# Gate vectors copied to all partitions by matmuls in place of GpSimd broadcasts, and small inputs loaded at the start

## The chip, the cores and the metric

The kernel runs on one core of a Trainium2 chip. The core has a tensor engine (PE; its weight loads are shown apart as PEld), a vector engine (DVE), a scalar engine (ACT), GpSimd (POOL) and a queue engine (SP) that here issues the large transfers. Each engine works through its own list of instructions in order and waits on semaphores for the others. The metric is the device time of one execution in microseconds.

## What is computed

256 tokens with 1024 channels, in float32, pass through two transformer blocks. The part that matters here is the modulation: six vectors of 1024 numbers for each layer come from a conditioning vector, and two of them are gates. A gate multiplies the result of a mixer or of a feed-forward network, channel by channel, before it is added to the tokens.

```python
mod = silu(c) @ w_ada + b_ada
sh1, sc1, g1, sh2, sc2, g2 = split(mod, 6)
x = x + g1 * mixer(modulate(x, norm1_g, sh1, sc1))
x = x + g2 * feed_forward(modulate(x, norm2_g, sh2, sc2))
```

The first block has one layer: a mixer of block attention and an mLSTM, then 32 experts. The second block has two layers: differential attention and then axial attention with grouped queries, each with a dense feed-forward network behind it. The differential attention needs one more number, lam, from four vectors of 64:

```python
lam = exp(sum(lq1 * lk1)) - exp(sum(lq2 * lk2)) + lam_init
```

## The kernel before

**Tiling.** Tokens lie on partitions in two tiles of 128; a product with weights takes activations transposed, 128 channels to a tile, and every operand is split in two exact halves, so that a float32 product is three matmuls (`mm3`). The halves of the activations are `hi` (ACT, line 593) and `lo` (POOL, line 596, from a tile `k` that DVE writes in line 595); those of the weights are `wh` (ACT, line 515) and `wl` (DVE, line 517), in at most four to six buffers. `dense` multiplies 512 columns of weights: eight steps of six matmuls into two banks of PSUM with the tag "g".

**Weights.** They come in units of 2 MiB, 5 slots in a ring, issued by SP in the order of use as slots come free (line 303). During the experts four further slots are there.

**Order of work.** Each engine's list is laid out at build time by a planner, which takes instructions by their place in the program text, lets one that is ready by its own model of the times go ahead of one that is not, and hands out buffers of a tag as they come free. Two calls bind it: `issue_after`, and `keep_in_program_order`, which pins an instruction behind the one that stands before it on the same engine in the text.

**Gates.** `gates` makes both gates of a layer in a tile `gm`: four rows, at partitions 0, 32, 64 and 96, with 512 numbers each, the other rows zero. `spread` copies each row to all 128 partitions, two rows for each gate, with four `partition_broadcast` instructions on POOL (line 497). It is called three times: in the first block, in layer 0 and in layer 1 of the second block, each time in `dense_work` between the mixer's products and `out_proj`, the product with the output weights, whose sums take all four banks "g". The gates are first read in `add_gated`, behind `out_proj` (lines 654 and 655). The first gate of the second block's layers stands in a buffer that held a value tile (`vh`, layer 0) or queries (`qT`, layer 1) before, and must wait for the attention's use of that. One more `partition_broadcast`, in line 1300, fills a gain for the experts' last group and is not touched.

**Layer 1 of the second block.** `axial_attention` has three products of 512 columns, for keys and values, and twice for queries. Behind each, `norm_rope` normalises the heads (line 1465 is the last to read the product's banks), rotates them (`rope_to`: products on DVE in lines 695 to 699, the sum and the difference on POOL in lines 697 and 700) and transposes them on PE (line 1474).

**Small inputs.** Five of the second block (`con_x`, `sub_g`, `lam`, `qk_g`, `grid`) are loaded by POOL in the middle of the first block (line 918), in text behind the mLSTM's gates. `lam` goes to all partitions, in a working tile of 1 KiB that must first come free; DVE sums the products on every partition (line 931), ACT takes the exponentials (line 933).

Of the kernel before, what the change touches and what calls it, by code (L numbers as in the profile page):

```python
# [19 lines left out]
T, D = 256, 1024  # L20
# [5 lines left out]
# columns of a unit of weights; the slots of their ring, and those beside it during the experts  # L26
UNIT = 4096
RING, RING2 = 5, 4
# the group of experts behind whose start the check for full queues comes
OVERFLOW_AT = 6  # L30
# how much of the mixers' attention goes beside their dense work, in steps more than there are: by layer of the second
# block; for the first block the steps of both
WEAVE = ((8, 0), (3, 0), (34, 52))
# (token tile, half) of the sums for GpSimd: of the second block, of the first
POOL_ADDS = ((0, 0), (1, 0))
POOL_A = ((0, 0),)
# how many splits stay behind the factors of a norm, by norm
BEHIND = (0, 4, 4, 0, 0)
# split weights held at a time, and the working tiles of the first mixer by size
AP, A1, A2 = 4, 6, 4  # L40
# shifts and scales computed with the vector engine: by layer and kind; the other modulation takes the tensor engine
COLS = ((0, 1), (1, 0), (1, 1))
# units of modulation after each unit of a mixer's weights, on the vector and on the tensor engine: of the first mixer,
# of the second
# [4 lines left out]
# the feed-forward network in two parts: their units of the first and of the second product  # L49
# [3 lines left out]
# columns of the constants: [128, C_N] for the whole program, [128, A_N] for the first block, [128, X_N] for the second  # L53
# [6 lines left out]
def constants():  # L60
    """Constants that depend on the shapes alone."""
# [30 lines left out]
def lay_out(i):  # L92
    """The inputs as the program reads them: slices, transposes and packing only."""
# [24 lines left out]
    def mcol(b, n1, n2):  # L118
        """biases of the shifts and scales and the gains, channels on partitions"""
        b = b.reshape(6, D)  # L120
        return np.concatenate([pc(b[0]), pc(b[1]), pc(n1), pc(b[3]), pc(b[4]), pc(n2)], 1)
# [7 lines left out]
    # outputs on rows: 512 of them to a unit  # L129
# [3 lines left out]
    # the first shift and scale by 256 channels: 128 shifts, their scales, and so on  # L133
# [28 lines left out]
    # by quarters of the columns  # L162
# [3 lines left out]
    # two heads' queries and keys to a unit, four heads' values  # L166
# [5 lines left out]
    o["lam"] = cc(np.concatenate([a["a_lam_q1_2"], a["a_lam_k1_2"], a["a_lam_q2_2"], a["a_lam_k2_2"]], 1))  # L172
# [12 lines left out]
def block_pair_kernel(ctx: ExitStack, tc: tile.TileContext, d, out):  # L185
# [12 lines left out]
    # working tiles by size: 1, 2 or 4 KiB to a partition  # L198
# [30 lines left out]
    # ---- the stream of weights: units of 2 MiB in the order of their use  # L229
# [51 lines left out]
    # the ring's slots: those of the last pool come first, and are the last before the second block's weights, which  # L281
    # wait for the first pool's
# [31 lines left out]
    # ---- constants and small inputs  # L314
    def bcast(src, offset, n):
        """n numbers of DRAM, the same on all partitions"""
        return bass.AP(tensor=src.tensor, offset=src.offset + offset, ap=[[0, 128], [1, n]])
# [14 lines left out]
    # the conditioning vectors  # L332
    se.activation(cs, cs, AF.Silu)

    def rsqrt(v, n):
        """1/sqrt(v), to float32's accuracy."""
# [4 lines left out]
        # with w = v y  # L341
# [15 lines left out]
    def rsqrts(vs):  # L357
        """1/sqrt(v) / RS for each v, one number a partition, to float32's accuracy."""
# [27 lines left out]
    def weave(*flows):  # L386
        """emits several flows (steps, their number) side by side"""
        live = [[0, n, steps] for steps, n in flows]
        while live:
            f = min(live, key=lambda f: (f[0] + 0.5) / f[1])  # L390
            f[0] += 1
            if next(f[2], live) is live:
                live.remove(f)

    def attention(n, ready, score, value, norm, turn, turn_ready=lambda: True):
        """steps of the attention by pairs of heads, each in n items: the scores of an item come ahead of the values of
        those before it, the transposition of a pair's result is put off behind scores of the next"""
# [26 lines left out]
    def ada(l, q, ps):  # L424
        """Two vectors of the modulation: psum rows 32j hold their pieces of 512"""
# [10 lines left out]
    def shift_scale(l, q, col, ps):  # L436
        """shift and gain * (1 + scale), channels on partitions: [128, 8 | 8]"""
# [10 lines left out]
    def ada_cols(l, q, cond, col):  # L448
        """a shift and a scale on the vector engine, outputs on partitions"""
# [12 lines left out]
    def cond_rows(b, dst):  # L462
        """a conditioning vector on all partitions"""
# [8 lines left out]
    def beside(steps, vfill, nv, fill, n_p):  # L472
        """8 steps with work of the modulation beside: units of the vector engine, and then those of the tensor engine"""
# [13 lines left out]
    def gates(l, m, ps):  # L487
        """the two gates, in rows 32j of m their pieces of 512"""
        po.memset(m, 0.0)
        po.dma_start(m[0:128:32, :], d["brow"][l])  # L490
        yield from ada(l, 2, ps)
        ve.tensor_add(m, ps, m)

    def spread(m, *gs):
        """the gates equal on all partitions"""
        for j in range(4):
            po.partition_broadcast(gs[j // 2][:, j % 2 * 512:(j % 2 + 1) * 512], m[32 * j:32 * j + 1, :])
# [6 lines left out]
    def behind():  # L504
        """the next splits are issued behind the norm's factors"""
# [5 lines left out]
    def split(w):  # L511
        """512 columns of weights as their two exact halves"""
# [7 lines left out]
    def mm3(ps, ah, al, bh, bl, first, last):  # L520
        """ps += a^T b, a and b in exact halves (the product of the two low halves is below float32's last place)"""
# [4 lines left out]
    def halves(tag="", pool=None):  # L526
        """activations, transposed, in exact halves: by 128 channels"""
        return tuple([mk(pool or parts[0], [128, T], F32R, f"{tag}{n}{k}") for k in range(DC)] for n in ("hi", "lo"))

    def dense(w, hi, lo, evict):  # L530
        """512 columns of weights: tokens on partitions"""
# [10 lines left out]
    def dense_t(w, hi, lo, evict, bank):  # L542
        """512 columns of weights: columns on partitions, 128 of them to a half bank"""
# [11 lines left out]
    def rows_into(w, ks, hi, lo, acc, first, last, lead=0, late=None):  # L555
        """acc[t][half] += a 128 rows of weights for each of ks, 1024 columns; the first tokens `lead` pieces ahead"""
# [21 lines left out]
    def turned(diag, evict, bank=psum, ks=range(0, DC, 2)):  # L578
        """the rows of x, each times its factor: evict(k, [128 channels, 256 tokens] in psum)"""
# [30 lines left out]
    def turn_into(hi, lo, gain, done, nh, k0=0):  # L610
        """a result, [128 tokens, t, nh, 128], to the exact halves of its transposes"""
# [10 lines left out]
    def out_proj(name, hi, lo, acc, done):  # L622
        """the product with a mixer's output weights, as the channels come"""
# [8 lines left out]
    def mean_square(src, junk):  # L632
        """one number a partition"""
# [4 lines left out]
    def diagonal(t, r, times):  # L638
        """the factors of 128 tokens on a diagonal"""
# [7 lines left out]
    def add_gated(t, acc, g, on_pool=POOL_ADDS, early=()):  # L647
        """x[t] += acc * g, by halves; its mean square, and EPS; in the tiles of the splits, but for `early` tokens, which come
        while those are in use"""
# [19 lines left out]
    def quotient_norm(v, den, nh, w, dst, ss=None):  # L669
        """v [128, nh, w] -> dst = v / den / rms(v / den), for den from 1 to the number of tokens; ss: sums of squares"""  # L670
# [5 lines left out]
    def head_norm(v, nh, w, dst, pre):  # L676
        """v [128, nh, w], times `pre` of each head -> dst = v / rms(v)"""
# [7 lines left out]
    def rope_to(dst, src, cs1, cs2, shape):  # L685
        """dst, src: (first halves, second halves); cs1, cs2: (cos, sin) for the first and for the second"""
# [15 lines left out]
    # =========================== first block, up to the experts ===========================  # L702
# [42 lines left out]
    # the conditioning vectors on all partitions, in the place of the gates that come later  # L745
# [3 lines left out]
    def modulated(u):  # L749
        """256 channels of the first modulation, and of the normalised tokens with it"""  # L750
# [14 lines left out]
    # queries and keys of the first attention: rotary embedding, transposed  # L765
# [8 lines left out]
    def store_k(dst, t, p2):  # L774
        """keys of two heads of 64 to a transposed tile, each with zeros in place of the other head"""
# [39 lines left out]
    def angles():  # L815
        """cos and sin of the given positions, arguments reduced to [-pi, pi]"""
# [24 lines left out]
    # the first product follows the channels as they come  # L841
# [21 lines left out]
    # gates of the mLSTM: heads on partitions, tokens along the free axis  # L863
# [5 lines left out]
    # rows h of these tiles are head h, the other rows stay zero  # L869
# [23 lines left out]
    # the running maximum that the second chunk starts from  # L893
# [12 lines left out]
    # as columns: [128 tokens, head]  # L906
# [9 lines left out]
    # small inputs of the second block  # L916
    def load(v, src):
        tc.keep_in_program_order(po.dma_start(v, src))
        return v

    con_x = load(mk(base, [128, X_CX], F32, "con_x"), d["const_x"][:, 0:X_CX])
    sub_g = load(mk(base, [128, 1], F32, "sub_g"), d["sub_g"])
    lamt = load(t1([128, 256]), bcast(d["lam"], 0, 256)).rearrange("p (a n) -> p a n", a=4)
    qk_g = load(mk(base, [128, 256], F32, "qk_g"), bcast(d["qk_g"], 0, 256)).rearrange("p (a n) -> p a n", a=2)
    grid = load(mk(base, [128, 256], F32, "grid"), d["const_x"][:, X_CX:X_N])

    LAM0 = 0.8 - 0.6 * math.exp(-0.3 * 0)
    ls = [mk(base, [128, 1], F32, f"ls{i}") for i in range(2)]
    for i in range(2):
        lj = t1([128, 64])  # L930
        ve.scalar_tensor_tensor(lj, lamt[:, 2 * i, :], 1.0, lamt[:, 2 * i + 1, :], op0=OP.mult, op1=OP.mult,
                                accum_out=ls[i])
        se.activation(ls[i], ls[i], AF.Exp)
    nlam = mk(base, [128, 1], F32, "nlam")
# [714 lines left out]
```

## Time and profile before

| | us |
|---|---|
| median of 3 runs | 1374.81 |
| lowest and highest | 1372.88 and 1378.33 |
| span of the profiled execution | 1375.5 |

The profile is of one execution, whose span, from its first to its last instruction, is 0.7 us above the median of the runs. Its page gives the busy time of each engine and a chain of work followed back from the end. [...] "issue" in brackets means that the engine waited for nothing that the profile shows.

### The profile page before, as it was taken

How to read it: one execution, taken by the hardware profiler on the slowest of the kernel's cores; microseconds unless marked ns; L12 is line 12 of the kernel's file. 1: busy time of each engine (PE TensorE's matmuls, PEld its weight loads, DVE VectorE, ACT ScalarE, POOL GpSimd, SP SyncE). 2: the span in 40 equal slices, each digit the busy share in tenths (PEclk: the TensorE clock that was granted, in tenths of full speed). 3: DMA queues.
4: the chain of work that ended last, by engine and by line, in shares of the span. 5: the costliest groups of instructions: out<-in, count | busy, mean ns of one | idle time of the engine just before them, and what ended most of it. 6: DMA issues, size and time to landing. Idle time of an engine off the chain costs nothing.

```text
span 1375.5 us, 19352 instructions
## 1 busy us (share of the span) xinstructions
PE 1116.8 (81%) x7505; PEld 813.4 (59%) x7505; DVE 680.8 (49%) x1598; ACT 485.4 (35%) x1046; POOL 160.6 (12%) x205
## 2 busy tenths in 40 slices
PE   5698998875656666575599999999995859999995
PEld 4486675421313222331377678989973646998994
DVE  7787896210202011111488777555553745655555
ACT  3254643100000000000356565554542525554552
POOL 2330000000000000000120103110123111310112
PEclk8799899978989897878899999999997989999998
DMA  9856887999999999989988739455365412844400
GB/s 389 352 200 254 339 316 327 429 425 426 425 428 427 426 427 425 424 363 428 425 329 319 279 120 373 181 192 198 149 255 211 180 61 107 338 184 184 184 32 31
DMA packets 29723, 397.51 MB, mean 289 GB/s; under 512 B 4156, under 2 KB 4556, under 8 KB 5560
## 3 DMA queue, kind: packets, MB, share of 16 engines
q1 hardware_dynamic: 28856, 395.22, 70.3%
q0 software_dynamic: 480, 0.96, 0.3%
q8 instruction: 61, 1.00, 0.3%
q14 instruction: 38, 0.31, 0.1%
q10 hardware_dynamic: 288, 0.02, 0.0%
HBM read 395.14 MB, written 1.05 MB: 288 GB/s over the span
## 4 chain that ended last, share of the span: by engine, by line
PE 39%; DMA 6%; DVE 5%; issue 4%; ACT 1%; POOL 1%; DVEq 0%; SPq 0%; ACTq 0%; POOLq 0%
PE b L524 6%; PE b L523 6%; PE b L522 6%; DMA w<-in_w_dram 6%; PE g L524 5%; PE g L522 5%; PE g L523 5%; DVE wl L517 1%; PE g L432 1%; PE b L1396 1%; PE b L585 1%; PE g L585 1%; PE b L1424 0%; PE b L1506 0%; PE b L1526 0%
## 5 line engine op out<-in xcount | busy, mean ns | idle before, releaser
L517 DVE TENSOR_TENSOR wl<-w,wh 128x512 fp32r<-128x512 f32 x440 | 309.6, 707 | 212.4 <-ACT wh L515 211.0
L515 ACT CAST wh<-w 128x512 fp32r<-128x512 f32 x440 | 270.3, 620 | 265.5 <-PE b L523 106.0
L1219 PE MATMUL g<-w,xg 128*32 128x512 f32 x1024 | 158.9, 754 | 97.8 <-DMA w<-in_w_dram 91.8
L522 PE MATMUL b<-hi,wh 128*128 128x256 f32 x704 | 199.4, 283 | 0.0
L523 PE MATMUL b<-lo,wh 128*128 128x256 f32 x704 | 199.2, 283 | 0.0
L524 PE MATMUL b<-hi,wl 128*128 128x256 f32 x704 | 199.2, 283 | 0.0
L1219 PEld LDWEIGHTS g<-w,xg 128*32 128x32 f32 x1024 | 33.0, 125 | 217.4 <-DMA w<-in_w_dram 114.7
L522 PEld LDWEIGHTS b<-hi,wh 128*128 128x128 f32 x704 | 135.2, 192 | 0.1
L523 PEld LDWEIGHTS b<-lo,wh 128*128 128x128 f32 x704 | 135.2, 192 | 0.1
L524 PEld LDWEIGHTS b<-hi,wl 128*128 128x128 f32 x704 | 135.2, 192 | 0.0
L1224 DVE TENSOR_TENSOR k<-g,k 128x512 f32<-128x512 f32 x8 | 5.5, 692 | 246.3 <-PE g L1219 246.3
L524 PE MATMUL g<-wh,lo 128*128 128x512 f32 x224 | 93.4, 419 | 18.4 <-POOL lo L596 18.3
L522 PE MATMUL g<-wh,hi 128*128 128x512 f32 x224 | 93.7, 425 | 8.8 <-ACT hi L593 5.9
L523 PE MATMUL g<-wl,hi 128*128 128x512 f32 x224 | 93.4, 417 | 0.0
L1236 PE MATMUL g<-w,k 128*32 128x256 f32 x1024 | 67.9, 403 | 17.4 <-DMA w<-in_w_dram 17.4
L1223 ACT ACTIVATE k<-g 128x512 f32<-128x512 f32 x8 | 4.8, 597 | 194.6 <-PE g L1219 194.5
L1606 POOL TENSOR_TENSOR fl<-k,fh 128x256 fp32r<-128x256 f32 x44 | 41.7, 950 | 270.3 <-ACT fh L1604 270.3
L522 PE MATMUL g<-wh,fh 128*128 128x512 f32 x176 | 68.5, 389 | 0.0
L523 PE MATMUL g<-wl,fh 128*128 128x512 f32 x176 | 68.5, 389 | 0.0
L524 PE MATMUL g<-wh,fl 128*128 128x512 f32 x176 | 68.5, 389 | 0.0
L524 PEld LDWEIGHTS g<-wh,lo 128*128 128x128 f32 x224 | 44.7, 201 | 29.8 <-POOL lo L596 20.9
L1236 PEld LDWEIGHTS g<-w,k 128*32 128x32 f32 x1024 | 31.9, 115 | 47.6 <-DMA w<-in_w_dram 19.6
(378 smaller groups left out, 1732.7 us busy)
## 6 DMA issues: line engine op xcount, KB each, us to landing
w<-in_w_dram SPq DMA_DIRECT2D x96, 2048.0 KB, 39.2
w<-in_ada_dram SPq DMA_DIRECT2D x36, 2048.0 KB, 7.9
w<-in_fin_dram SPq DMA_DIRECT2D x22, 2048.0 KB, 8.3
w<-in_fout_dram SPq DMA_DIRECT2D x10, 2048.0 KB, 7.6
w<-in_w_in_dram SPq DMA_DIRECT2D x7, 2048.0 KB, 11.5
w<-in_aqkv_dram SPq DMA_DIRECT2D x6, 2048.0 KB, 10.4
w<-in_bqkv_dram SPq DMA_DIRECT2D x3, 2048.0 KB, 8.7
w<-in_w_out_dram SPq DMA_DIRECT2D x2, 2048.0 KB, 9.7
```

Of the source, the lines that this page charges most:

```text
L432: te.matmul(ps[32 * j:32 * j + 32, :], cs[:, i:i + 1].to_broadcast([128, 32]), w[:, a, j, :], start=k == 0, stop=k == DC - 1)
L515: se.copy(wh, w)
L517: ve.tensor_sub(wl, w, wh.bitcast(F32))
L522: te.matmul(ps, ah, bh, start=first, stop=False, skip_group_check=True)
L523: te.matmul(ps, ah, bl, start=False, stop=False, skip_group_check=True)
L524: te.matmul(ps, al, bh, start=False, stop=last, skip_group_check=True)
L585: te.matmul(ps[:, a, t * 128:(t + 1) * 128], x[t][:, k * 128:(k + 1) * 128], diag[t], start=True, stop=True)
L1219: te.matmul(ps[32 * j:32 * j + 32, :], xg[:, k, c0:c0 + CAP], up(nm, k, j), start=k == 0, stop=k == DC - 1)
L1224: ve.tensor_mul(sg, pss[1], sg)
L1236: te.matmul(ps[32 * j:32 * j + 32, :], hT[:, f, 32 * j:32 * j + 32], down(q, f, j), start=f == 0, stop=f == 3)
L1396: te.matmul(ps[:, a, :], qTs[p][:, h, t * 128:(t + 1) * 128], kTs[p % 3][:, 2 * h + a, :], start=True, stop=True)
L1606: po.tensor_sub(w, sg, h.bitcast(F32))
```

## The change

`spread` uses the tensor engine: a column of the identity matrix, repeated 128 times, is the stationary operand, so that every output partition gets one row of `gm`; the result goes through a bank "g" and a copy by ACT. The five loads move up to a place behind `angles`, ahead of the first product; `lam` is laid out with its four vectors as columns of 64 numbers, is loaded to 64 partitions, in a small tile of its own, and its sums come from one matmul with ones. Comments and docstrings are taken out, too.

```diff
     def spread(m, *gs):
         for j in range(4):
-            po.partition_broadcast(gs[j // 2][:, j % 2 * 512:(j % 2 + 1) * 512], m[32 * j:32 * j + 1, :])
+            ps = psum_g()
+            te.matmul(ps, ident[:, 32 * j:32 * j + 1].to_broadcast([128, 128]), m, start=True, stop=True)
+            se.copy(gs[j // 2][:, j % 2 * 512:(j % 2 + 1) * 512], ps)
...
+    def load(v, src):
+        tc.keep_in_program_order(po.dma_start(v, src))
+        return v
+
+    con_x = load(mk(base, [128, X_CX], F32, "con_x"), d["const_x"][:, 0:X_CX])
+    sub_g = load(mk(base, [128, 1], F32, "sub_g"), d["sub_g"])
+    lamt = load(mk(paa, [64, 4], F32, "lam"), d["lam"])
+    qk_g = load(mk(base, [128, 256], F32, "qk_g"), bcast(d["qk_g"], 0, 256)).rearrange("p (a n) -> p a n", a=2)
+    grid = load(mk(base, [128, 256], F32, "grid"), d["const_x"][:, X_CX:X_N])
+
     for u in range(4):
         if u == 1:
             angles()
         modulated(u)
...
-    con_x = load(mk(base, [128, X_CX], F32, "con_x"), d["const_x"][:, 0:X_CX])
-    sub_g = load(mk(base, [128, 1], F32, "sub_g"), d["sub_g"])
-    lamt = load(t1([128, 256]), bcast(d["lam"], 0, 256)).rearrange("p (a n) -> p a n", a=4)
-    qk_g = load(mk(base, [128, 256], F32, "qk_g"), bcast(d["qk_g"], 0, 256)).rearrange("p (a n) -> p a n", a=2)
-    grid = load(mk(base, [128, 256], F32, "grid"), d["const_x"][:, X_CX:X_N])
-
     LAM0 = 0.8 - 0.6 * math.exp(-0.3 * 0)
-    ls = [mk(base, [128, 1], F32, f"ls{i}") for i in range(2)]
+    lp, one = small(2)[0:64], small(1)[0:64]
+    po.memset(one, 1.0)
     for i in range(2):
-        lj = t1([128, 64])
-        ve.scalar_tensor_tensor(lj, lamt[:, 2 * i, :], 1.0, lamt[:, 2 * i + 1, :], op0=OP.mult, op1=OP.mult,
-                                accum_out=ls[i])
-        se.activation(ls[i], ls[i], AF.Exp)
+        ve.tensor_mul(lp[:, i:i + 1], lamt[:, 2 * i:2 * i + 1], lamt[:, 2 * i + 1:2 * i + 2])
+    psl = psum()
+    te.matmul(psl[:, 0:2], one.to_broadcast([64, 128]), lp, start=True, stop=True)
+    ls = mk(base, [128, 2], F32, "ls")
+    se.activation(ls, psl[:, 0:2], AF.Exp)
     nlam = mk(base, [128, 1], F32, "nlam")
-    ve.tensor_sub(nlam, ls[1], ls[0])
+    ve.tensor_sub(nlam, ls[:, 1:2], ls[:, 0:1])
     ve.tensor_scalar(nlam, nlam, -LAM0, None, op0=OP.add)
-    po.tensor_scalar(sub_g, sub_g, 1.0 - LAM0, None, op0=OP.mult)
+    tc.keep_in_program_order(po.tensor_scalar(sub_g, sub_g, 1.0 - LAM0, None, op0=OP.mult))
```

## Rows read from the trace of the kernel before

**Rows 1.** The page: its span, and the busy time of each engine (share of the span, instructions).

```profile
span 1375.5 us, 19352 instructions
PE 1116.8 (81%) x7505; PEld 813.4 (59%) x7505; DVE 680.8 (49%) x1598; ACT 485.4 (35%) x1046; POOL 160.6 (12%) x205
```

**Rows 2.** Stretches of time: their length, then busy time and instructions of PE, PEld, DVE, ACT and POOL, the granted clock, the DMA engines' share and GB/s. Here stages of the second block's two layers.

```profile
760.00:834.00 74.00, 73.06 (x395) 51.99 (x393) 57.17 (x162) 42.05 (x118) 10.51 (x16) 1.00 0.57 220
...
1041.00:1058.00 17.00, 0.78 (x3) 0.34 (x3) 3.14 (x6) 1.84 (x4) 1.89 (x3) 0.63 0.41 176
...
1113.00:1130.00 17.00, 2.69 (x13) 1.89 (x11) 3.33 (x8) 2.35 (x4) 2.14 (x3) 0.72 0.32 123
...
1165.00:1340.00 175.00, 173.72 (x1303) 163.84 (x1296) 98.60 (x172) 94.53 (x178) 28.12 (x31) 1.00 0.49 190
```

**Rows 3.** POOL's instructions in order of time in the attention of layer 1: start and duration, line, operation, tiles, and idle time before with what ended it.

```profile
1038.53 0.74 POOL L596 TENSOR_TENSOR lo<-k,hi 128x256 fp32r<-128x256 f32 x1
1049.10 0.80 POOL L497 PARTITION_BROADCAST g<-gm  x1 [9.83 <-issue]
1056.91 5.30 POOL L596 TENSOR_TENSOR lo<-k,hi 128x256 fp32r<-128x256 f32 x7 [7.01 <-issue]
1068.36 1.16 POOL L497 PARTITION_BROADCAST g<-gm  x1 [6.14 <-issue]
1076.44 0.81 POOL L697 TENSOR_TENSOR rt<-k,k 128x128 f32<-128x128 f32 x1 [6.92 <-DVE wl L517]
...
1089.93 0.79 POOL L697 TENSOR_TENSOR rt<-k,k 128x256 f32<-128x256 f32 x1 [11.38 <-DVE k L696]
...
1111.73 0.73 POOL L700 TENSOR_TENSOR rt<-k,k 128x256 f32<-128x256 f32 x1 [0.69 <-DVE k L699]
1118.32 0.80 POOL L497 PARTITION_BROADCAST qT<-gm  x1 [5.87 <-issue]
1128.66 0.71 POOL L697 TENSOR_TENSOR rt<-k,k 128x256 f32<-128x256 f32 x1 [9.54 <-issue]
```

**Rows 4.** Waits of PE over the whole span: whose instruction, who was waited for, then the total in us, how many times, and the longest.

```profile
PE b L1474 <- POOL rt L700: 19.6, 5, 14.4
PE g L524 <- POOL lo L596: 18.3, 3, 16.2
```

**Rows 5.** DVE's instructions in order of time: the last tile `k` for `lo`, the first difference's operands behind the product for keys, and the last product of the rotation behind the second broadcast's stretch.

```profile
1045.21 0.54 DVE L595 TENSOR_SCALAR k<-b,col 128x256 f32<-128x256 f32 x1 [0.71 <-ACT hi L593]
```

```profile
1074.72 0.29 DVE L696 TENSOR_TENSOR k<-rt,ax10s 128x128 f32<-128x128 f32 x1
```

```profile
1113.93 0.41 DVE L699 TENSOR_TENSOR k<-rt,ax01s 128x256 f32<-128x256 f32 x1
```

**Rows 6.** The chain of work in order of time (start, us, what) where it passes through PE: the third matmul of the product for keys and values, a float32 matmul of 256 columns (four of them), one matmul of a split product with 512 columns, and 64 float32 matmuls of 512 columns, which run four side by side, each on 32 columns of the array.

```profile
1039.32 0.50 PE g L524
```

```profile
722.54 0.86 PE b L1396 x4
...
724.10 0.23 PE g L522
```

```profile
826.96 7.00 PE g L432 x64
```

**Rows 7.** ACT: the first copy that reads the finished product for keys and values (in order of time), and a copy of a whole bank (one line of the kernel: count and shortest, median and longest duration in ns).

```profile
1068.18 0.37 ACT L1488 COPY vb<-g 128x256 f32<-128x256 f32 x1
```

```profile
L1021 ACT COPY vx<-g x2: 588/588/589, 164.5 to 165.2; 128x512 f32<-128x512 f32 x2
```

**Rows 8.** Short stretches, columns as in Rows 2: behind the two long idle times of layer 1, around the load of `lam`, and at the spread of the first block.

```profile
1058.00:1062.00 4.00, 4.00 (x10) 3.14 (x10) 1.29 (x1) 1.07 (x2) 4.00 (x6) 0.50 0.02 4
...
1130.00:1134.00 4.00, 3.89 (x13) 3.34 (x14) 0.78 (x2) 0.71 (x2) 0.06 (x1) 0.50 0.00 0
```

```profile
108.00:112.00 4.00, 3.99 (x17) 3.50 (x18) 2.97 (x11) 3.46 (x10) 0.00 (x0) 0.50 0.77 262
112.00:116.00 4.00, 4.00 (x26) 2.05 (x27) 2.17 (x5) 2.25 (x8) 0.00 (x0) 0.81 0.65 279
185.00:189.00 4.00, 1.35 (x14) 1.02 (x12) 3.67 (x11) 2.02 (x6) 3.06 (x4) 0.95 1.02 438
```

**Rows 9.** The sum over `lam` in line 931: what ended DVE's idle time before it (us, times); and the first matmul behind that on PE, in order of time.

```profile
  DMA k<-in_lam_dram: 5.7, 1
```

```profile
108.01 1.12 PE L969 MATMUL b<-va,pT 128*128 128x64 f32 x4 [4.57 <-ACT pT L965]
```

**Rows 10.** The start: DVE's first instruction, and the queue of POOL's transfers over the whole span (packets, MB, share of 16 engines' span).

```profile
9.35 1.22 DVE L757 SCALAR_TENSOR_TENSOR w<-w,g 128x1024 f32<-128x1024 f32 x1 [9.35 <-DMA w<-in_ada_dram]
```

```profile
q0 software_dynamic: 480, 0.96, 0.3%
```

**Rows 11.** POOL in order of time around the spread of layer 0, and the stretch of the experts' weights, columns as in Rows 2.

```profile
780.37 1.48 POOL L497 PARTITION_BROADCAST vh<-gm  x2 [18.61 <-PE g L524]
...
795.33 0.33 POOL L697 TENSOR_TENSOR rt<-k,k 128x64 f32<-128x64 f32 x1 [10.37 <-DVE k L698]
```

```profile
300.00:600.00 300.00, 192.86 (x1582) 79.67 (x1581) 44.19 (x110) 17.31 (x37) 0.00 (x0) 0.86 0.99 419
```

**Rows 12.** Layer 1: the last reads by DVE of the banks of the first two products, and the first matmul of `out_proj` on PE, in order of time.

```profile
1075.32 0.42 DVE L1465 TENSOR_TENSOR rt<-g,s 128x256 f32<-128x256 f32 x1
```

```profile
1090.93 0.68 DVE L1465 TENSOR_TENSOR rt<-g,s 128x512 f32<-128x512 f32 x1
```

```profile
1108.29 0.50 PE L522 MATMUL g<-wh,ohi 128*128 128x512 f32 x1 [0.46 <-ACT ohi L603]
```

More of the change, by code (lines that the diff above doesn't have):

```diff
@@ L171, in lay_out @@
     o["awo"] = rows(a["a_w_o_2"][0])
-    o["lam"] = cc(np.concatenate([a["a_lam_q1_2"], a["a_lam_k1_2"], a["a_lam_q2_2"], a["a_lam_k2_2"]], 1))
+    o["lam"] = cc(np.concatenate([a["a_lam_q1_2"], a["a_lam_k1_2"], a["a_lam_q2_2"], a["a_lam_k2_2"]], 0).T)
     o["sub_g"] = cc(a["a_subln_g_2"].T)
@@ L914, in block_pair_kernel @@
     ve.tensor_copy(gcol[:, 4, :], pst2[:, 0:4])
-    def load(v, src):
-        tc.keep_in_program_order(po.dma_start(v, src))
-        return v
-    con_x = load(mk(base, [128, X_CX], F32, "con_x"), d["const_x"][:, 0:X_CX])
-    sub_g = load(mk(base, [128, 1], F32, "sub_g"), d["sub_g"])
-    lamt = load(t1([128, 256]), bcast(d["lam"], 0, 256)).rearrange("p (a n) -> p a n", a=4)
-    qk_g = load(mk(base, [128, 256], F32, "qk_g"), bcast(d["qk_g"], 0, 256)).rearrange("p (a n) -> p a n", a=2)
-    grid = load(mk(base, [128, 256], F32, "grid"), d["const_x"][:, X_CX:X_N])
     LAM0 = 0.8 - 0.6 * math.exp(-0.3 * 0)
-    ls = [mk(base, [128, 1], F32, f"ls{i}") for i in range(2)]
+    lp, one = small(2)[0:64], small(1)[0:64]
+    po.memset(one, 1.0)
     for i in range(2):
-        lj = t1([128, 64])
-        ve.scalar_tensor_tensor(lj, lamt[:, 2 * i, :], 1.0, lamt[:, 2 * i + 1, :], op0=OP.mult, op1=OP.mult,
-                                accum_out=ls[i])
-        se.activation(ls[i], ls[i], AF.Exp)
+        ve.tensor_mul(lp[:, i:i + 1], lamt[:, 2 * i:2 * i + 1], lamt[:, 2 * i + 1:2 * i + 2])
[3 more added lines that the diff above has]
+    se.activation(ls, psl[:, 0:2], AF.Exp)
     nlam = mk(base, [128, 1], F32, "nlam")
-    ve.tensor_sub(nlam, ls[1], ls[0])
+    ve.tensor_sub(nlam, ls[:, 1:2], ls[:, 0:1])
     ve.tensor_scalar(nlam, nlam, -LAM0, None, op0=OP.add)
-    po.tensor_scalar(sub_g, sub_g, 1.0 - LAM0, None, op0=OP.mult)
+    tc.keep_in_program_order(po.tensor_scalar(sub_g, sub_g, 1.0 - LAM0, None, op0=OP.mult))
     nmx, den, outs = {}, {}, {}
```

## The prediction

> **What bounds the kernel now.** I read the page first: the span is 1375.5 us, and PE is busy for 81% of it while POOL is busy for 12% [rows 1]. An engine that works 12% of the time can still stop the others, so I next went through the stretches of time, stage by stage. From 300 to 600 us the DMA engines are busy for 0.99 of the time and PE for two thirds: the experts wait for weights [rows 11]. The stretches of the second block are PE's: 73.06 of 74 us in the attention of layer 0, 173.72 of 175 in the last feed-forward network [rows 2]. Two stretches in the attention of layer 1 stand out, in which nothing is the bound: from 1041 to 1058 PE is busy for 0.78 of 17 us, from 1113 to 1130 for 2.69 of 17, and no other engine is busy for more than 3.4 [rows 2]. The totals of PE's waits put both down to POOL: one wait of 16.2 us for `lo`, one of 14.4 for the rotation's sum [rows 4]. POOL's own list shows why. It waits 9.83 us before a broadcast and 7.01 before the subtraction behind it, 5.87 and 9.54 around the next, each time with no releaser ("issue"), while the broadcast itself takes 0.80 [rows 3]. The same subtraction follows an idle time of 11.38 us without delay when no broadcast stands before it: it starts when DVE's product ends [rows 3]. So a change between the broadcast and other POOL work costs 6 to 10 us each way, and everything behind it in POOL's list pays.
>
> [...]
>
> **The change part by part.** *First stretch of layer 1.* The product for keys and values had its third matmul at 1039.32, and a matmul of 512 columns follows the one before in 0.23 us [rows 6]; the other 45 take 10.4 us, so it could end at 1049.7. The last `k` is ready at 1045.75 and its `lo` 0.74 later [rows 5, 3], three pieces ahead of need. In fact the product was first read at 1068.18 [rows 7]: 18.5 us later, of which 16.2 are the wait and the rest is the half clock behind it, 0.50 from 1058 to 1062 [rows 8]. I take 18, between 16.2 and 18.5. *The broadcast at 1068.36:* the operands of the rotation's first difference are there at 1075.01, POOL starts at 1076.44 [rows 5, 3]: 1 us, between 0 and 1.4. *Second stretch:* the last operand is ready at 1114.34 [rows 5]; with 0.73 for the sum [rows 3] PE could go on at 1115.1, and it went on after 1130.0, when POOL's pair at 1128.66 was done [rows 3]. That is 15 us, and the clock behind it is 0.50 for 4 us with PE busy for 3.89 [rows 8]: up to 2 more, of which I count half, since this stage is a chain of short waits. 16, between 14.4 and 17.
>
> *The load of `lam`.* DVE stands 5.7 us for it, PE's next matmul comes after 4.57 of idle time, and the clock then is 0.50 and 0.81 for 4 us each, with PE busy throughout [rows 9, 8]: 2.0 and 0.8 us more. With the load at the start nobody waits: 6.6, between 4.6 and 7.4. This lies ahead of the experts, whose stream of weights is full from its first units on [rows 11] and starts earlier with what precedes it, so I pass the gain on whole. POOL's scaling of `sub_g`, now pinned in the text's order, has nothing but the small clearing before it. The new sum for `lam` (two tiny products, a matmul, one exponential in place of two sums and two exponentials) I cost at nothing: it is shorter than what it replaces and waits for nothing that is late.
>
> *The loads at the start.* POOL's queue moved 0.96 MB in 0.3% of the span, 4.1 us of all 16 engines [rows 10]. The loads that move are about 0.27 MB: 1.2 us, at a time when DVE waits 9.35 us for the first unit of weights [rows 10] and follows it from there. They share the engines with that unit; 0.7 us, between 0 and 1.2. SP's queue is not touched; in POOL's list nothing else is due before the first `lo`.
>
> *The matmuls and copies.* Four float32 matmuls of 256 columns took 0.86 us [rows 6], so one of 512 takes 0.43, and a spread 1.7. The 64 of 512 columns in 7.00 us, four side by side, give 0.44 [rows 6]. A copy of a bank on ACT is 0.59 [rows 7], a spread 2.4. In the first block PE is busy for 1.35 of 4 us at that place, ACT for 2.02 [rows 8]: the matmuls are hidden, the copies nearly; 0.5 us, between 0 and 2.4 (if the copies stand ahead of the weights' splits in ACT's list and the cover is gone). In layer 0 PE has no idle time to hide them [rows 2]: 1.7 at least, 4.1 if the copies come on top, 2 taken. Its broadcasts cost nothing before, since POOL's next work waited for DVE [rows 11]. In layer 1 I take 2.5, between 0 and 4.1: PE has gaps there, but the copies stand among exponentials. The new wait is for banks "g": `out_proj` now needs them back from the copies, and behind its first matmul on PE stand the attention's.
>
> [...]
>
> *Sum:* 18 + 1 + 16 + 6.6 = 41.6 gained, 0.7 + 0.5 + 2 + 2.5 = 5.7 added: 35.9 less than 1375.5 is 1339.6, and with the 0.7 by which this execution lies above the median of 1374.81, **1339**. The bounds: at best 44.3 gained and 1.7 added, 1332; at worst 35.2 gained and 11.8 added, 1351.
>
> **The rivals.** *Banks held too long.* The planner may put a spread's matmuls of layer 1 into an early gap of PE, since `gm` is ready before the first product. Those for the first gate then keep two of the four banks until the queries' buffer is free, and the later products must each wait until the one before has been read: for keys and values that was at 1075.7, 7.5 us after its end [rows 12, 7]. Twice 7.5 on top is 1354. For it: the planner did move broadcasts for the second gate that far ahead [rows 3]. Against it: PE has hardly a gap there once `lo` comes in time.
>
> *The stretches are not the broadcasts' doing.* If some other cause holds POOL, both remain; only `lam` is gained: 1375.5 - 6.6 + 5.7 - 0.7 is 1374, no change. Against it is the subtraction that follows 11.38 us of idleness at once [rows 3].
>
> *Slower: the clock of the last feed-forward network.* It runs 175 us with PE busy for 173.72, at 1.00 [rows 2]. With 34 us of rest gone before it, the chip might grant less: at 0.80 it would take 219 us, and the result would be 1383. It decides from 0.83 on, where the 36 us are used up. Against it speaks that the lower clocks are found behind idle stretches [rows 8], not behind busy ones.
>
> **How the numbers follow.** A difference under 0.5%, 6.9 us, can't be told from none by measuring this kernel. Chances: the forecast, from 1332 to 1351, 0.70; held banks, 1351 to 1360, 0.15; no effect, 0.05; the lower clock, 0.04; 0.06 for a new layout of the lists that moves the result outside these without changing its sign. Faster is 0.91, the same 0.05, slower 0.04. The range reaches from 1331 to 1356: the bounds of the sum and the held banks at their price.
>
> **What would show it.** In the profile after, `spread`'s line has matmuls of 0.4 us and copies of 0.6 and no broadcast; line 1300's is the only one left. PE's waits for `lo` and for the rotation's sum fall from 16.2 and 14.4 to about 1, the two stretches are filled, and the clock behind them stays at 1.00. DVE's wait for `lam` is gone and its first instruction starts at 9.4 to 10.6. I am wrong if waits of over 5 us for a "g" bank or for ACT's copies stand in layer 1, if POOL still rests without a releaser before `lo`, or if the experts' stage does not start some 5 us earlier.

## The result

| | us, median | to before, with its 95% interval |
|---|---|---|
| before | 1376.57 | |
| changed | 1341.28 (4 runs, 1340.11 to 1343.10) | 0.9742 (0.972 to 0.9764) |

The changed kernel is faster by 2.6%, some 35 us. The forecast was 1339, the range 1331 to 1356. The ratios here and below leave disturbed runs out, so they need not be the quotient of two medians.

### The profile after

The page (span; busy time of each engine, share and instructions), beside [rows 1]: the busy times hardly move, the span is 36.8 us shorter.

```profile
span 1338.7 us, 19377 instructions
PE 1111.9 (83%) x7531; PEld 813.6 (61%) x7531; DVE 679.3 (51%) x1596; ACT 491.3 (37%) x1057; POOL 152.9 (11%) x194
```

Stretches of time with the columns of [rows 2]: the attention of layer 0, the two stretches of layer 1 (the product for keys and values, then the end of the queries), the last feed-forward network.

```profile
753.00:827.00 74.00, 73.48 (x382) 52.91 (x384) 53.86 (x148) 42.79 (x120) 7.64 (x12) 1.00 0.54 205
1036.00:1053.00 17.00, 16.27 (x72) 13.11 (x70) 14.75 (x37) 10.06 (x19) 6.73 (x9) 1.00 0.77 316
1076.00:1093.00 17.00, 13.33 (x67) 9.43 (x66) 11.57 (x31) 8.81 (x22) 2.94 (x4) 0.90 0.00 0
1128.00:1303.00 175.00, 173.85 (x1306) 163.78 (x1299) 98.87 (x172) 94.42 (x178) 28.26 (x31) 1.00 0.49 190
```

In the stretches where PE was busy for 0.78 and 2.69 of 17 us [rows 2] it is busy for 16.27 and 13.33. The tensor engine's granted clock (1.00 is full speed) over the second is 0.90, so it did not stay at 1.00 as forecast. The last network runs at clock 1.00 as before. PE's waits for POOL there are now

```profile
PE b L1479 <- POOL rt L702: 3.4, 3, 1.3
PE g L526 <- POOL lo L598: 2.6, 2, 1.4
```

in place of 19.6 and 18.3, with longest waits of 1.3 and 1.4 in place of 14.4 and 16.2 [rows 4]. POOL's list in layer 1 (start, duration, line, operation, idle time before it):

```profile
1034.14 0.74 POOL L598 TENSOR_TENSOR lo<-k,hi 128x256 fp32r<-128x256 f32 x1
1035.44 1.44 POOL L598 TENSOR_TENSOR lo<-k,hi 128x256 fp32r<-128x256 f32 x2 [0.56 <-DVE k L597]
1038.11 4.88 POOL L598 TENSOR_TENSOR lo<-k,hi 128x256 fp32r<-128x256 f32 x5 [1.23 <-DVE k L597]
1052.03 0.57 POOL L699 TENSOR_TENSOR rt<-k,k 128x128 f32<-128x128 f32 x1 [9.04 <-DVE k L698]
```

No idle time without a releaser is left in layer 1: what POOL waits for is DVE's products, and it starts when they end.

Where the 36.8 us of the two profiled executions were gained and lost, by the start of the same matmul in both (its place in words):

| matmul | before | after | gained so far |
|---|---|---|---|
| first of the first product's input | 16.08 | 19.07 | -3.0 |
| first transposition of a mixer result | 125.00 | 120.69 | 4.3 |
| first of the mLSTM's scores | 166.61 | 159.86 | 6.8 |
| first of the router | 219.64 | 212.01 | 7.6 |
| first score of layer 0 | 720.13 | 713.02 | 7.1 |
| first transposition of the next network's shifts | 835.19 | 830.83 | 4.4 |
| first transposition of layer 1's heads | 1077.72 | 1053.58 | 24.1 |
| last transposition of layer 1's shifts (its end) | 1170.64 | 1133.97 | 36.7 |

### The profile page after: what moved, and what is told of

It is laid out like the page before. It is cut to its first block, busy times and chain, and to the rows that moved or that the text cites. A ratio compares the mean times of both kernels' runs of the same rounds, so it can differ in the third digit from the quotient of the medians.

```text
span 1338.7 us, 19377 instructions
## 1 busy us (share of the span) xinstructions
PE 1111.9 (83%) x7531; PEld 813.6 (61%) x7531; DVE 679.3 (51%) x1596; ACT 491.3 (37%) x1057; POOL 152.9 (11%) x194
## 4 chain that ended last, share of the span: by engine, by line
PE 41%; DMA 6%; DVE 3%; issue 2%; POOL 2%; ACT 1%; SPq 0%; DVEq 0%; ACTq 0%; POOLq 0%
PE b L526 6%; PE b L525 6%; PE b L524 6%; DMA w<-in_w_dram 6%; PE g L524 5%; PE g L526 5%; PE g L525 5%; PE g L432 1%; PE b L1401 1%; DVE wl L519 1%; POOL x L657 1%; PE b L1511 1%; PE b L1531 1%; PE g L587 1%; PE b L1429 1%
## 5 line engine op out<-in xcount | busy, mean ns | idle before, releaser
L1224 PE MATMUL g<-w,xg 128*32 128x512 f32 x1024 | 152.1, 726 | 106.4 <-DMA w<-in_w_dram 99.4
L1231 ACT COPY k<-b 128x512 f32<-128x512 f32 x8 | 4.7, 586 | 152.1 <-PE b L786 152.1
L455 DVE SCALAR_TENSOR_TENSOR w<-w,g 128x1024 f32<-128x1024 f32 x48 | 58.6, 1226 | 0.1
```

Of the source, the lines that this page charges most:

```text
L455: ve.scalar_tensor_tensor(w[:, s], w[:, s], 1.0, cond, op0=OP.mult, op1=OP.mult, accum_out=part[:, 4 * u + j:4 * u + j + 1])
L1224: te.matmul(ps[32 * j:32 * j + 32, :], xg[:, k, c0:c0 + CAP], up(nm, k, j), start=k == 0, stop=k == DC - 1)
```

## The experiments

| run | us, median | to before, with its 95% interval |
|---|---|---|
| e1, matmuls alone | 1343.24 | 0.9752 (0.9727 to 0.9777) |
| e2, loads alone | 1376.76 | 0.9983 (0.9961 to 1.0005) |
| e3, matmuls in layer 1 only | 1338.03 | 0.9724 (0.9701 to 0.9747) |
| e4, loads later | 1338.64 | 0.9723 (0.9701 to 0.9746) |
| e5, broadcasts last | 1341.83 | 0.9740 (0.9710 to 0.9770) |
| e6, one broadcast | 1359.06 | 0.9881 (0.9851 to 0.9911) |
| e7, both savings | 1338.45 | 0.9724 (0.9698 to 0.9749) |
| e8, broadcasts last, loads later | 1334.64 | 0.9704 (0.9680 to 0.9728) |
| e9, matmuls twice | 1349.02 | 0.9799 (0.9778 to 0.9821) |
| e10, two loads later | 1340.41 | 0.9738 (0.9714 to 0.9762) |
| e11, later loads alone | 1370.02 | 0.9961 (0.9947 to 0.9975) |

### Is it the broadcast, or what stands around it?

**e6, one broadcast.** The changed kernel with one matmul of layer 1 turned back:

```diff
-    def spread(m, *gs):
+    def spread(m, *gs, by_pool=()):
...
+            if j in by_pool:
+                po.partition_broadcast(v, m[32 * j:32 * j + 1, :])
+                continue
...
-            spread(gm, *g1)
+            spread(gm, *g1, by_pool=(2,) if l else ())
```

> The changed kernel with one of the four matmuls of layer 1 replaced by a broadcast (the first half of the second gate), which the planner puts behind the first lo. Theory (each stretch costs by the change of code there and back, whatever number of broadcasts stands in it): the whole first stretch comes back, a wait for lo of some 16 us, and the time is 1341.3 + 17, 1358. Rival (four broadcasts cost 35 us, so one costs 9): 1350. Rival (the broadcast isn't the cause): 1341.

1359.06: 18 us more than the changed kernel. POOL's list and PE's wait:

```profile
1033.92 0.74 POOL L602 TENSOR_TENSOR lo<-k,hi 128x256 fp32r<-128x256 f32 x1
1044.40 0.80 POOL L499 PARTITION_BROADCAST g<-gm  x1 [9.73 <-issue]
1052.21 5.31 POOL L602 TENSOR_TENSOR lo<-k,hi 128x256 fp32r<-128x256 f32 x7 [7.00 <-issue]
```

```profile
PE g L530 <- POOL lo L602: 18.9, 4, 16.1
```

One instruction of 0.80 us brings back 9.73 and 7.00 us of idle POOL and a wait of 16.1, as in [rows 3, 4]. A price for each broadcast (1350) is out.

The brackets name no releaser, but the trace holds a record of what stands there. Each of these idle times begins with two instructions `MODIFY_POOL_CONFIG` of POOL's sequencer, put down to the line of the instruction that comes after it: in the kernel before at 1039.5 for the broadcast at 1049.10, and at 1049.8 for the subtraction at 1056.91 [rows 3]. The first two rows show these two places, the third the same line of code in e5 (next) over the whole span (count; shortest, median and longest in ns; first and last start):

```profile
L497 POOLq MODIFY_POOL_CONFIG  x2: 12/12/12, 1039.5 to 1039.5; - x2
```

```profile
L596 POOLq MODIFY_POOL_CONFIG  x2: 129/129/129, 1049.8 to 1049.9; - x2
```

```profile
L497 POOLq MODIFY_POOL_CONFIG  x6: 7/8/37, 101.8 to 1099.2; - x6
```

Line 497 has 12 of them in the kernel before, for six groups of broadcasts, and 6 in e5, for three. Over all lines there are 30 in the kernel before, 18 in e5, 10 in e6 and 6 in the changed kernel. So what is paid for is a change of POOL's configuration; what the engine does during these 6 to 10 us the trace does not show.

**e5, broadcasts last.** The kernel before with no matmul and no load moved, only an order:

```diff
-            po.partition_broadcast(gs[j // 2][:, j % 2 * 512:(j % 2 + 1) * 512], m[32 * j:32 * j + 1, :])
+            v = po.partition_broadcast(gs[j // 2][:, j % 2 * 512:(j % 2 + 1) * 512], m[32 * j:32 * j + 1, :])
+            if pin:
+                tc.keep_in_program_order(v)
...
-            spread(gm, *g1)
+            spread(gm, *g1, pin=l == 1)
```

> The kernel before with one edit: in layer 1 the four broadcasts are pinned behind the last rotation in POOL's list, in all else they stay, and no matmul is added. Theory (it is not the broadcast that costs but the changes of POOL's code in front of lo and of the rotation): both long waits of layer 1 go, and neither layer pays for matmuls; from 1343.2 of the matmuls alone, less 3.4 in layer 0 and 3.4 to 5.4 in layer 1, 1334 to 1336. Rival (the broadcasts, behind the attention's use of the queries' buffer, come too late for the gated sum, and a change of code of up to 10 us then stands in front of it): 1345 or more.

The median is 1341.83, so the order alone gives, within the noise, what the whole change gives, but 6 to 8 us less than I expected. POOL's list in layer 1:

```profile
1097.84 1.10 POOL L702 TENSOR_TENSOR rt<-k,k 128x256 f32<-128x256 f32 x1 [0.36 <-DVE k L701]
1105.10 1.62 POOL L497 PARTITION_BROADCAST qT<-gm  x2 [6.16 <-issue]
1106.58 1.46 POOL L497 PARTITION_BROADCAST g<-gm  x2
1127.72 1.29 POOL L657 TENSOR_TENSOR x<-x,wl 128x512 f32<-128x512 f32 x1 [19.68 <-DVE wl L656]
```

The four broadcasts stand together behind the last rotation; one change of 6.16 us leads in, the way back lies in 19.68 us in which POOL waits for DVE. The rival (too late for the gated sum) is out. In its profiled execution layer 0 (from its first score to the transpositions behind it) takes 115.0 us and the stage from there to the end of layer 1's transpositions 302.0, against 117.8 and 303.1 in the changed kernel: the second block is faster by 3.9. I had expected 6.8 to 8.8 there, 3.4 in layer 0 and 3.4 to 5.4 in layer 1, and found 2.8 and 1.1: the matmuls cost the second block less than the time they take on PE. The rest is in what the sum started from, e1, whose profiled execution came to layer 0 4.3 us earlier than that of the kernel before, although its lists are the same up to the first spread (below).

### The two parts

**e1, matmuls alone.** `spread` as changed, loads left in line 918.

> The kernel before with the new spread alone; the five loads stay where they were. Theory (the two parts add up, and the loads' part is the smaller): the loads' part is worth 9.6 us around the load of lam less 3.0 at the start, so this takes 1341.3 + 6.6, 1348. DVE still waits some 5.7 us for lam, and its first instruction starts at 9.4. Rival (what the loads gain is lost again at the experts' stream of weights): 1341.

**e2, loads alone.** The loads as changed, the broadcasts back.

> The changed kernel with the broadcasts put back in all three places; the loads stand at the start. Theory: 1376.6 - 6.6, 1370; PE's waits for lo and for the rotation's sum in layer 1 are 16 and 14 us again. Rival (the loads' part is lost at the experts' stream): 1376. A second rival (the long waits came from the late loads of layer 1's constants and not from the broadcasts): below 1345, without the two waits.

The matmuls alone give 34 us, the loads alone 2 (between 5 and none): within the noise they add up. e2 keeps both long waits of layer 1 (total, times, longest), so the late loads did not cause them:

```profile
PE b L1477 <- POOL rt L700: 19.9, 5, 14.3
PE g L524 <- POOL lo L596: 18.4, 4, 15.5
```

But by these runs the loads are worth a third of what I had worked out. The size is loosely known: e2's profiled execution is 6.2 us shorter than that of the kernel before. **e11, later loads alone**, takes their cost at the start away (the place is that of e4):

> The changed kernel with all broadcasts put back and the five loads behind the first product: only the loads differ from the kernel before, and they cost nothing at the start. Theory by the profiled executions (7.1 us gained in the first block with the loads at the start, and 3.0 back from the start): 1375.5 - 10, 1366. Rival (the profiled execution of the kernel before met the lower clock twice around the load of lam, as other executions of the same lists do not, so the load is worth some 2 us less what the start costs, plus 3.0 now): 1371.

1370.02, 5.4 us less than before (3.4 to 7.3), at the rival. Why the profiled executions showed more is seen in e1. In it the late load still holds DVE and PE, but for less than in [rows 9]:

```profile
105.64 0.23 DVE L933 SCALAR_TENSOR_TENSOR k<-k 128x64 f32<-128x64 f32 x1 [4.27 <-DMA k<-in_lam_dram]
```

```profile
107.02 0.71 PE L971 MATMUL b<-va,pT 128*128 128x64 f32 x4 [3.15 <-ACT pT L967]
```

Up to the first spread e1's instruction lists are those of the kernel before on every engine, and yet its first score of the mLSTM starts at 162.23 and not at 166.61. The load lands 1 us earlier and DVE waits 1.4 less; most of the rest is the clock. The same stretch (columns as in [rows 2]) in the kernel before, in e1, in the changed kernel and in e11:

```profile
144.00:162.00 18.00, 15.50 (x57) 11.73 (x56) 14.71 (x45) 11.37 (x20) 0.00 (x0) 0.72 0.64 271
```

```profile
142.00:158.00 16.00, 13.44 (x59) 9.89 (x58) 13.11 (x42) 11.37 (x20) 0.00 (x0) 0.89 0.72 308
```

```profile
140.00:158.00 18.00, 15.43 (x65) 11.75 (x66) 15.25 (x48) 12.58 (x23) 0.00 (x0) 0.91 0.68 277
```

```profile
140.00:158.00 18.00, 17.08 (x61) 13.29 (x62) 14.73 (x45) 10.41 (x16) 0.00 (x0) 0.72 0.64 260
```

0.72 comes with the late load and without it (e11), 0.9 likewise (e1 with it, the changed kernel without). So that clock is no effect of the load, and some 2.5 of the 7 us that the changed profile shows gained ahead of the experts are not the change's. What decides the clock there is open.

**e4, loads later.** The five loads move behind the first product in the text:

```diff
     emit(first)
     for _ in mixed(0, range(8)):
         pass
+    con_x = load(mk(base, [128, X_CX], F32, "con_x"), d["const_x"][:, 0:X_CX])
...
+    grid = load(mk(base, [128, 256], F32, "grid"), d["const_x"][:, X_CX:X_N])
```

> The changed kernel with the five loads moved from the start to a place behind the first product, some 55 to 70 us after the start, where the DMA engines are no longer full. Theory (at the start they cost 3.0 us, since they delay the tokens by 4 us, and nothing needs them before 100 us): 1338.3, with DVE's first instruction at 9.4 and no wait for lam. Rival (the start's delay is taken up by a later wait of the first block for weights): 1341.

1338.64, 2.6 us less, which the intervals of the times do not separate from none. The profiles show that the start's price is real: PE's first matmul for the first product's input starts at 16.1 to 16.3 us in the seven executions without loads at the start and at 19.1 to 19.4 in the five with all of them, and e4 comes to layer 0's first score 2.8 us before the changed kernel (710.26 against 713.02). ACT's first work on the tokens is in the kernel before, the changed kernel, e4 and e10:

```profile
10.51 1.06 ACT L635 ACTIVATE k<-x 128x1024 bf16<-128x1024 f32 x1 [2.48 <-DMA x<-in_x_dram]
```

```profile
14.60 1.06 ACT L637 ACTIVATE k<-x 128x1024 bf16<-128x1024 f32 x1 [6.09 <-DMA x<-in_x_dram]
```

```profile
10.59 1.06 ACT L637 ACTIVATE k<-x 128x1024 bf16<-128x1024 f32 x1 [2.46 <-DMA x<-in_x_dram]
```

```profile
12.50 1.06 ACT L637 ACTIVATE k<-x 128x1024 bf16<-128x1024 f32 x1 [4.28 <-DMA x<-in_x_dram]
```

**e10, two loads later.** Only `qk_g` and `grid` move behind the first product.

> The changed kernel with only con_x, sub_g and lam at the start (17.5 KB together), and the two loads of 128 KB each (qk_g and grid) behind the first product. Theory (the two large loads take the start's 3.0 us): the first of DVE's instructions at 9.4 and the time of the later loads, 1338.5. Rival (any load of POOL's queue at this place costs, by its packets and not its bytes): DVE's first instruction at 11.4 again, and 1341.

1340.41 lies between the two and, with an interval of 3.3 us to a side, decides nothing. By the profile neither holds as it stands: the tokens come 2.0 us later than before by the three small loads, and 2.1 more by the two large ones, although these have fifteen times the bytes. DVE's first instruction starts at 11.03, and at 11.35 in the changed kernel. What does go with the tokens' delay is the count of packets: POOL's queue has 192 in the first 20 us of the changed kernel and 96 in e10 (packets, MB, share of 16 engines):

```profile
q0 software_dynamic: 192, 0.28, 8.5%
```

```profile
q0 software_dynamic: 96, 0.02, 0.5%
```

That is the rival's idea, on two points; no run changes the packets alone. The DMA engines from 8 to 12 us (the two last columns: share, GB/s) in the kernel before, the changed kernel and e10:

```profile
8.00:12.00 4.00, 0.00 (x0) 0.00 (x0) 2.65 (x5) 1.36 (x4) 0.00 (x0) 0.89 1.03 420
```

```profile
8.00:12.00 4.00, 0.00 (x0) 0.00 (x0) 0.65 (x1) 0.51 (x1) 0.00 (x0) 1.00 0.74 149
```

```profile
8.00:12.00 4.00, 0.00 (x0) 0.00 (x0) 0.97 (x1) 0.23 (x1) 0.00 (x0) 1.00 0.76 276
```

The engines are full before; with the loads they are idle for a quarter of these 4 us and move 149 or 276 GB/s. What they wait for the views don't show.

### What the matmuls cost

**e3, matmuls in layer 1 only.**

```diff
+            if not by_pe:
+                po.partition_broadcast(v, m[32 * j:32 * j + 1, :])
+                continue
...
-            spread(gm, *g1)
+            spread(gm, *g1, by_pe=l == 1)
```

> The changed kernel with broadcasts in the first block and in layer 0, and matmuls in layer 1 alone. Theory (the gain is all in layer 1; in layer 0 POOL has time for the broadcasts and PE has none for the matmuls): the 3.4 us of eight records of 0.43 us come back, 1338. Rival (the matmuls of layer 0 only fill time that PE would have waited): 1341. Rival (the broadcasts of layer 0 now delay the rotation): over 1345.

1338.03, at the theory. The interval of the time reaches nearly to 1341, so what decides is layer 0, which takes 115.4 us in its profile, against 117.8 changed and 115.1 before. In the first block the matmuls cost next to nothing. From the mLSTM's first score to the router the five profiles with these matmuls done once take 52.0 to 52.2 us, all at clock 1.00. With broadcasts it is 51.7 at 1.00 (e3), 53.0 to 53.2 at 0.97 (five executions) and 54.1 at 0.94 (e7). So the matmuls cost 0.5 us where the clock is the same, and six of the seven executions with broadcasts took longer than any of the five. PE's list shows what hides the matmuls. In e3, at the place of the spread, it has idle time:

```profile
180.02 0.25 PE L1023 MATMUL g<-con,k 36*128 36x36 f32 x1 [0.54 <-DVE k L1022]
182.24 0.71 PE L1067 MATMUL b<-vx,pr 128*128 128x130 f32 x4 [1.97 <-DVE pr L1060]
```

In the changed kernel the spread stands ahead of that place, and these waits are gone:

```profile
178.33 3.60 PE L498 MATMUL g<-k,con 128*128 128x512 f32 x8
```

**e9, matmuls twice.**

```diff
+            for _ in range(2):
                 te.matmul(ps, ident[:, 32 * j:32 * j + 1].to_broadcast([128, 128]), m, start=True, stop=True)
```

> The changed kernel with each of the twelve matmuls done twice into the same bank. Theory (a float32 matmul of 512 columns takes 0.86 us, two records of 0.43, and PE has no idle time to hide it in the second block): 3.4 us more in layer 0 and 3.4 in layer 1, nothing in the first block, 1341.3 + 6.9, 1348. Rival (in layer 1 they fill time in which PE would wait anyway): 3.4 in layer 0 and under 1 in layer 1, 1345. Rival (0.43 us for one matmul, as the prediction had it): 1.7 in each layer, 1344.7, with layer 0 longer by 1.7.

1349.02, at the theory's 1348, but not by its places. In the profile, of an execution of 1351.13, layer 0 takes 3.3 us more than in the changed kernel (121.1), the stage behind it 2.2 more (305.4), and the first block 3.0 up to the router, where I expected nothing: the first four matmuls had used up the idle time. Another 2.2 us, between the router and layer 0's first score, have no explanation here. The instructions of that line (count; shortest, median, longest in ns) in the changed kernel and in e9:

```profile
L498 PE MATMUL g<-gm,con x16: 591/592/1061, 786.7 to 1088.8; 128*128 128x512 f32 x16
```

```profile
L499 PE MATMUL g<-gm,con x32: 590/592/697, 791.8 to 1100.9; 128*128 128x512 f32 x32
```

Eight matmuls of the second block leave 16 records, sixteen leave 32: a float32 matmul has two. PE's list in layer 0 gives their pace:

```profile
786.67 1.88 PE L498 MATMUL g<-gm,con 128*128 128x512 f32 x4
788.38 0.60 PE L786 MATMUL b<-con,rt 128*128 128x128 f32 x4
```

Four records, two matmuls, and the next instruction starts 1.71 us later: 0.43 for a record, 0.86 for a matmul.

### Both together

**e7, both savings** (e3 and e4):

> Matmuls in layer 1 alone, and the five loads behind the first product. Theory (the two savings lie in different stages and add up): 1338.0 - 2.6, 1335.4. Rival (what the start gives is lost again at the experts' stream): 1338.

**e8, broadcasts last, loads later** (e5's order and e4's place):

> Broadcasts in all three places, those of layer 1 pinned behind the last rotation, and the five loads behind the first product: no matmul for the gates at all. Theory: 1338.6 of the later loads, less 3.4 in layer 0 and 3.4 to 5.4 in layer 1, 1330 to 1332, the fastest of all. Rival (the broadcasts come too late for the gated sum of layer 1): 1340 or more.

e7 shows no sum: 1338.45, like e3 and e4 each. The intervals are some 3.4 us to a side, so a missing 2.6 can't be told from a bad draw. Its profiled execution, at 1338.57 close to the median, shows one: it comes to the mLSTM's first score 2.5 us before e3's (157.50 against 160.01), and loses this again by the router, with the same lists as e3, in 54.1 us at clock 0.94 against 51.7 at 1.00. For its other runs this stays open. e8 has the lowest median of all, 1334.64, 3% below the kernel before and 6.6 us below the changed one, though its interval overlaps with those of e3, e4 and e7, and it is 2.6 above the upper end of what was expected. Against e4 its profile gains 2.4 us in layer 0 and 2.7 in layer 1, where I had put 3.4 and 3.4 to 5.4, and gives back 1.1 between the mLSTM's first score and the router. It has no matmul for the gates.

## Why the prediction was right, point by point

- **What held PE in layer 1: right.** The two long waits are gone. e6 brings one back with a single broadcast, e5 removes both with the broadcasts kept: the change of POOL's configuration ahead of `lo` and of the rotation was the price, and two `MODIFY_POOL_CONFIG` stand in the trace at each. The rival that the stretches had another cause is out. Before a broadcast POOL's idle time without a releaser was 9.83, 6.14 and 5.87 us in the kernel before [rows 3], 9.73 in e6 and 6.16 in e5; behind one it was 7.01 and 9.54 [rows 3] and 7.00 in e6. That it is a change of code, as the expectations of e5 and e6 put it, was my guess: the traces show the two records and the idle time.
- **First stretch and the broadcast behind it, 18 + 1:** the gain grows by 19.8 from the layer 0 row to layer 1's first transposition.
- **Second stretch and the spread, 16 - 2.5 = 13.5:** it grows by 12.5 from there to the end of layer 1's transpositions, with the clock at 0.98 over that stage in the changed kernel. At 1.00 throughout, the way from layer 0's end to that of layer 1's transpositions takes 2.7 us more with the matmuls (e4, 302.4) than with the broadcasts last (e8, 299.7), close to the 2.5 taken for the spread.
- **Layer 0, 2:** 2.7, inside its bounds. The bounds themselves rested on a mistake: "one of 512 takes 0.43, and a spread 1.7" took a record for a matmul. Four records of 256 columns in 0.86 us [rows 6] were two matmuls, and so the 64 there are 32. With two records to a matmul, 512 columns take 0.86 us at clock 1.00 (four records in 1.71 us, layer 0 of the changed kernel), and a spread is 3.4 us of PE. The total survived, since the first block hid its share and both layers a part: the spread's 3.4 us cost layer 0 2.3 to 2.8 us (117.7 to 117.8 in the five profiles with the matmuls done once, 115.0 to 115.4 in the seven with broadcasts).
- **First block's spread, 0.5:** changed and e3 differ there by 0.5 at the router (212.01 against 211.66, from 159.86 and 160.01), by idle time of 2.5 us. Right at the same clock, but the idle time is used up (e9), and at the clock that six of seven executions with broadcasts met there the matmuls come out ahead by 1 to 2 us.
- **The loads at the start, 0.7 (0 to 1.2): wrong.** 3.0 in the profile, 2.6 by e4. The step that failed is "the loads that move are about 0.27 MB: 1.2 us": it shares out the engines' time by bytes. 17.5 KB cost half of it (e10). DVE's first instruction starts at 11.35 and not, as was to show it, at 9.4 to 10.6.
- **`lam`, 6.6 (4.6 to 7.4):** 5.4 by e11, inside the bounds, though its interval reaches below and takes in the 6.6. The 6.6 were one execution's waits and clock; e1's waits for the same load are 4.27 and 3.15, not 5.7 and 4.57. With the start's 3.0 the loads' part is 2 us net (e2) and not 5.9.
- **Passing the prelude's gain on whole:** 7.6 at the router, 7.1 at layer 0. Right.
- **Held banks (1354): in place, but short.** In layer 1 the first gate's two matmuls end at 1076.3 and are copied at 1091.2 (ACT's two copies into the queries' buffer). For 15 us two banks are gone, as the rival said; but the planner put them behind the last matmul of the second product for queries, when no product was left to wait, and only the second gate's matmuls did (start, duration, line, idle time before):

```profile
1074.55 1.88 PE L498 MATMUL g<-gm,con 128*128 128x512 f32 x4
...
1086.18 1.12 PE L498 MATMUL g<-gm,con 128*128 128x512 f32 x2 [1.35 <-DVE rt L1470]
1087.98 1.85 PE L498 MATMUL g<-gm,con 128*128 128x512 f32 x2 [0.68 <-ACT g L499]
```

  2.0 us instead of 15.
- **The last network's clock (1383): out.** 1.00 and 173.85 us of 175.

So the forecast's 35.9 met a median 35.3 us lower, but the sum was closer than its terms, and that is partly luck: too little for the start (by 2.3) and for layer 0 (0.7), too much for `lam` (1.2 by e11's median), and a first block that in the profiled execution also met a better clock. Shown are the cause in layer 1, the price of a matmul and the price of the loads at the start; open are what the DMA engines wait for there and what sets the clock around 150 us and in the stretch behind it.

## What to carry to other kernels

The broadcast on GpSimd cost here what stands around it: 9.73 and 7.00 us of idle time around one of 0.80 (e6). In another kernel, look for idle time without a releaser before such an operation and before the next ordinary one, for `MODIFY_POOL_CONFIG` at its start, and ask who waits for that engine there. Moving the operation behind the last instruction that others wait for may give the whole gain (1341.83 in e5, 1341.28 with the whole change); here that costs PE nothing, where the matmuls cost 2.3 to 2.8 us in layer 0 and 1.1 (e5) to 2.7 (e8) in layer 1. Small loads were not free while the DMA engines were full (share 1.03 from 8 to 12 us in the kernel before), few as their bytes were: 17.5 KB delayed the tokens by 2.0 us (e10). And a wait's worth should be read from more than one execution: DVE's wait for `lam` was 5.7 us in one [rows 9] and 4.27 in another (e1).

## What was not expected of the hardware

- A broadcast of 0.80 us between two subtractions on GpSimd brought 9.73 and 7.00 us of idle time (e6), each opened by two `MODIFY_POOL_CONFIG`; four broadcasts in a row brought one change on the way in, 6.16 us (e5).
- A float32 matmul leaves two records; 512 columns took 0.43 us each at clock 1.00.
- Three loads of 17.5 KB together, issued by POOL from 2.5 us on, delayed the tokens by 2.0 us, five of 0.27 MB by 4.1; the DMA engines' share fell from 1.03 to 0.76 and 0.74.
- Two executions with the same lists differed by 4.4 us at 160 us, by a load's landing and by the clock (0.72 against 0.89 for some 17 us).
